# First layer's shift and scale vectors from TensorE column tiles, and no element-wise products on GpSimd, in a four-layer decoder trunk

## The chip, the cores and the metric

One core of a Trainium2 chip runs the whole program in one launch. The metric is device microseconds of one execution, the median of 3 runs.

## The reference, cut to what matters

Four layers work on 256 tokens of 1024 features. Each layer has a token mixer (layers 0 and 3: attention in a window of 128 with rotary positions; layer 1: gated linear attention; layer 2: forgetting attention) and a SwiGLU feed-forward part. Ahead of each part the tokens are normalised and modulated by vectors that come from one conditioning vector `c` and a 1024 x 6144 matrix per layer:

```
mod = silu(c) @ ada_w[i] + ada_b[i]
sh1, sc1, g1, sh2, sc2, g2 = split(mod, 6)
h = rmsnorm(x, gain) * (1 + sc1) + sh1
x = x + g1 * mixer(h)
h = rmsnorm(x, gain') * (1 + sc2) + sh2
x = x + g2 * swiglu(h)
```

So each layer has six modulation vectors of 1024, each the product of `silu(c)` with a 1024 x 1024 block (4 MB). All arithmetic is float32.

## The kernel before, in words

**Stream of weights.** All weights arrive in the order of one list (`items`, L1144), mostly 1 MB at a time, through SyncE's DMA queue into a ring of `RAW` = 5 tiles named `raw` (L94, L180). The load of an item waits until the item five places ahead of it has been used up. There are two kinds. A `w` item is a weight chunk: ScalarE casts it to `wh` (L195) and VectorE takes the remainder `wl = raw - wh` (L197), in two pieces each. An `a` item holds the columns of one modulation vector for 256 features, transposed, so that one feature is one partition row of 1024 numbers.

**Modulation vectors (`ada_pieces`, L201).** An `a` item has two pieces of 128 features. A piece is normally one VectorE instruction (L217): multiply the 128 x 1024 tile by `cact` (`silu(c)` on all partitions), sum along the row, add the bias. For the pieces in `POOL_ADA` (L60, layer 0 only: 18 of its 40 pieces of vectors 0 to 4) GpSimd multiplies (L212), ScalarE sums (L214) and VectorE adds the bias (L215).

**Matrix products** are made of three float32r matmuls each (`mm3`, L258: high x high, high x low, low x high).

**The order at the start (layer 0).** `ORDER0` (L56) lists the first 30 items: `w` chunks of the mixer, `h`, `s`, `g`, `H`, `S` the items of vectors 0 (shift), 1 (scale), 2 (gate), 3 (second shift), 4 (second scale). `first_chunks` (L695) sums the squares of `x` (ScalarE L405, additions on GpSimd L416), takes the norm with small TensorE products (L309, L322, L332), and then works in four rounds `r`. A round forces the items of shift and scale for two of the eight feature tiles, makes the scale column `A` (L361), the two tiles of `h` (VectorE L435 `tk`, ScalarE L437 `hh`, VectorE L430 `hl`), and runs the matmuls of these two tiles for the first two weight chunks (keys, values) as far as their weights are there. In this kernel the first chunk is item 0 and the second item 8.

**The rest of the mixer.** Keys and four groups of queries get the rotary positions (`rope`, L613: VectorE L622, L623, L625, then an addition, L631 for keys and L629 for queries). `ROPE_ADD` (L58) puts these additions on GpSimd in layer 0 and on VectorE in layer 3. Attention (`attn_heads`, L529) runs as a background generator between the matmuls: scores (TensorE L559), masks and minimum (VectorE L572), exponentials (ScalarE L577), division (VectorE L547 and ScalarE L545), transposes (L600), values (TensorE L589, two heads at output partitions 0 to 63 and 64 to 127). GpSimd copies the sink columns (L569, L570). The remaining items of the stream are used up between the matmuls, in shares (`tick`, L226). `out_proj` and the feed-forward part follow.

`Tile`, the layer under this code, draws the waits, and may put an instruction that is ready earlier ahead of others on its engine.

Of the kernel before, what the change touches and what calls it, by code (L numbers as in the profile page):

```python
# [13 lines left out]
AF = mybir.ActivationFunctionType  # L14
ALU = mybir.AluOpType
PSUM = bass.MemoryType.PSUM

P = 128
D = 1024
KT = D // P  # L20
S = 256
# [5 lines left out]
GH = 4  # L27
# [4 lines left out]

CONST_COLS = [
    ("ident", 128), ("ones", 2), ("eps", 1), ("gain", DEPTH * 2 * KT), ("ada_b", DEPTH * 48),
    ("fin", KT), ("hnorm", 2), ("bgate", GH), ("bf", 1),
]
CONST2_COLS = [
    ("cos", NB * HD), ("sin", NB * HD), ("swamask", 3 * P), ("foxmask", 3 * P), ("scan", S),
# [14 lines left out]
WIDE = KT * (256 + 16)  # L53
RAW = 5
MIX_POOL = ((), (), (), ())
ORDER0 = "wshshshhwswwwgwwgggSwHSwHSSHHw"  # L56
BG_SWA = ((1.2, -6.5, 4.5), (0.63, 2.0, 1.6))
ROPE_ADD = (('gpsimd', 'gpsimd'), ('vector', 'vector'))  # L58
EARLY = 2
POOL_ADA = {(0, 0): (0, 1, 2, 4, 5), (0, 1): (7,), (0, 2): (1, 3, 4), (0, 3): (0, 1, 2, 4, 5), (0, 4): (1, 3, 4, 7)}  # L60
CUTS = (2, 2, 2)
OUT_POOL = ()
FFN_POOL = ()
# [80 lines left out]
class Builder:  # L144
# [56 lines left out]
    def ada_pieces(self, it, raw):  # L201

        nc = self.nc
        layer, nt = it[1]
        mod = self.mod[layer]
        bias = self.c("ada_b")[:, layer * 48:(layer + 1) * 48]

        def piece(i):
            w = raw[:, i * D:(i + 1) * D]
            col, b = mod[:, nt + i:nt + i + 1], bias[:, nt + i:nt + i + 1]  # L210
            if (nt + i) % KT in POOL_ADA.get((layer, nt // KT), ()):
                nc.gpsimd.tensor_tensor(out=w, in0=w, in1=self.cact, op=ALU.mult)  # L212
                s = self.t(self.small, [P, 1], "adac", bufs=2)
                nc.scalar.activation(w, w, AF.Copy, accum_out=s)  # L214
                nc.vector.tensor_tensor(out=col, in0=s, in1=b, op=ALU.add)  # L215
            else:
                nc.vector.tensor_tensor_reduce(out=w, in0=w, in1=self.cact, scale=1.0, scalar=b,  # L217
                                               op0=ALU.mult, op1=ALU.add, accum_out=col)
        return [lambda: piece(0), lambda: piece(1)]


    def start_chunk(self, ticks):
# [472 lines left out]
    def first_chunks(self):  # L695

        nc = self.nc
        self.A, self.late = None, []
        self.st.cap = self.st.widx[EARLY]
        self.per_tick = 0.0  # L700
        for k in range(KT):
            self.x_done(k)
        self.stat_start(self.acc)
        self.stat_end()
        self.tc.keep_in_program_order(nc.scalar.dma_start(self.const2, self.a["const2"]))
        rbs = self.t(self.small, [P, S], "rbs", bufs=1)
        nc.scalar.copy(rbs, self.spread(self.y))
        hs = hh, hl = self.h_alloc()
        A = self.t(self.small, [P, KT], "A", bufs=2)
        sh = self.mod[0][:, :KT]  # L710
        outs, ws, todo = [], [], []
        for r in range(4):
            self.st.force_ada(0, (0, 1), r)
            self.mod_cols(0, 0, 2 * r, 2 * r + 2, A)
            self.h_tiles(range(2 * r, 2 * r + 2), rbs, A, sh, hh, hl)
            while len(ws) < EARLY and (r == 3 or self.st.pos[f"i0_{len(ws)}"] < self.st.done):
                c = len(ws)
                ws.append([x.rearrange("p (k n) -> p k n", k=KT) for x in self.st.get(f"i0_{c}")])
                self.st.cap = self.st.widx[EARLY]
                outs.append(self.banks(("mm", "s")[c])[0])  # L720
                todo.append(0)
            for c, (wh, wl) in enumerate(ws):
                for k in range(todo[c], 2 * r + 2):
                    for m in range(2):
                        sl = slice(m * P, (m + 1) * P)
                        self.mm3(outs[c][m][:, :S], hh[:, k, sl], hl[:, k, sl], wh[:, k], wl[:, k],
                                 k == 0, k == KT - 1)
                todo[c] = 2 * r + 2
        return hs, [[o[:, :S] for o in out] for out in outs]
# [482 lines left out]
    def build(self):  # L1212
        nc, tc, ctx = self.nc, self.tc, self.ctx
        pool = lambda n: ctx.enter_context(tc.tile_pool(name=n, bufs=1))
        cp = pool("const")
        self.wpool = pool("w")
        self.hpool = pool("h")
        self.small = pool("small")
        self.psum = ctx.enter_context(tc.tile_pool(name="ps", bufs=1, space=PSUM))

        self.x = self.t(cp, [P, KT, S], "x")
        self.const = self.t(cp, [P, CONST_W], "const")
        self.const2 = self.t(cp, [P, CONST2_W], "const2")
        self.cact = self.t(cp, [P, D], "cact")
        self.mod = [self.t(cp, [P, 48], f"mod{l}") for l in range(DEPTH)]
        self.gla_wg = self.t(cp, [16, GH * P], "gla_wg")
        self.gla_masks = self.t(cp, [P, 7, P], "gla_masks", U8)

        crow = self.t(self.hpool, [P, KT, S], "hh", bufs=1).rearrange("p k n -> p (k n)")[:1, :D]
        nc.sync.dma_start(crow, self.a["c"])  # L1230
        nc.sync.dma_start(self.const, self.a["const"])
        nc.sync.dma_start(self.x, self.a["x"])
        self.st = Stream(self, self.items())
        self.st.issue()
        one = self.t(self.small, [P, S], "fc", bufs=2)[:1, :P]
        nc.vector.memset(one, 1.0)
        for i in range(2):
            ps = self.ps("t")
            sl = slice(i * 512, (i + 1) * 512)
            nc.tensor.matmul(ps, one, crow[:, sl], start=True, stop=True)  # L1240
            nc.scalar.activation(self.cact[:, sl], ps, AF.Silu)

        mixers = [self.swa, self.gla, self.fox]
        for l in range(DEPTH):
            with tc.tile_pool(name=f"mix{l}", bufs=1, reuse_waits="tile") as mp:
                self.layer = l
                self.done_k = 0
                oh = self.t(mp, [P, KT, S], "oh", F32R)
                ol = self.t(mp, [P, KT, S], "ol", F32R)
                self.cuts, self.on_pool = CUTS[0], MIX_POOL[l]  # L1250
                mixers[l % 3](l, oh, ol, mp)
                self.cuts, self.on_pool = CUTS[1], OUT_POOL
                self.out_proj(l, oh, ol, self.mod[l][:, 2 * KT:3 * KT])
            self.cuts, self.on_pool = CUTS[2], FFN_POOL
            self.ffn(l)
        self.final_tile(KT - 1)
        stat = self.ps("o")
        self.stat = [stat[:, b:b + 1] for b in range(NB)]
        self.stat_end(self.acc)
        for i, ps in enumerate(self.final):  # L1260
            o = self.t(self.wpool, [P, WIDE], "raw", bufs=RAW)[:, :512]
            b, half = divmod(i, 2)
            y = self.y[:, b:b + 1]
            if b:
                nc.scalar.activation(o, ps, AF.Copy, scale=y)
            else:
                nc.vector.tensor_scalar(out=o, in0=ps, scalar1=y, scalar2=None, op0=ALU.mult)
            (nc.scalar if b else nc.sync).dma_start(
                self.out[b * P:(b + 1) * P, half * 512:(half + 1) * 512], o)
# [3 lines left out]
def _chunks(w, cols):  # L1273

    k, n = w.shape
    return w.reshape(k // P, P, n // cols, cols).transpose(2, 1, 0, 3).reshape(n // cols, P, -1)
# [8 lines left out]
def _colmajor(v):  # L1285

    return v.reshape(-1, P).T


def _layout(i):  # L1290
    f = np.float32
    a = {}
    a["x"] = i["x"][0].T.reshape(KT, P, S).transpose(1, 0, 2)
    a["c"] = i["c"].reshape(1, D)
    ada = i["ada_w"].reshape(DEPTH, D, 6, D).transpose(0, 2, 3, 1)
    a["ada"] = ada.reshape(DEPTH * 6, 4, 2, P, D).transpose(0, 1, 3, 2, 4).reshape(DEPTH * 6, 4, P, 2 * D)
    gu = i["ffn_w_gu"].reshape(DEPTH, KT, P, 2, FT, P)[:, :, :, :, :2]
    gu = gu.transpose(0, 4, 2, 1, 3, 5).reshape(DEPTH, 2, P, KT * 2 * P)
    gt = i["ffn_w_gu"].reshape(DEPTH, 2, KT // 2, P, 2, FT // 2, 2 * P)[:, :, :, :, :, 1:]
# [8 lines left out]
    w = i["gla_w_in"][0]  # L1308
# [6 lines left out]
    w = i["fox_w_in"][0]  # L1315
# [6 lines left out]
    c, c2 = np.zeros((P, CONST_W), f), np.zeros((P, CONST2_W), f)  # L1322

    def put(name, v):
        lo, hi = COFF[name] if name in COFF else C2OFF[name]
        (c if name in COFF else c2)[:v.shape[0], lo:hi] = v
    put("ident", np.eye(P, dtype=f))
    put("ones", np.tile(np.array([[1.0 / D, 1.0 / 256]], f), (P, 1)))
    put("eps", np.full((P, 1), EPS, f))
    put("gain", _colmajor(i["norm_gain"]))  # L1330
    put("ada_b", _colmajor(i["ada_b"]))
# [19 lines left out]
    s, t = np.arange(P)[:, None], np.arange(P)[None, :]  # L1351
# [22 lines left out]
```

## Time and profile before

| | |
|---|---|
| median of 3 runs (range) | 1269.9 us (1268.44 to 1271.39) |
| the profiled execution | 1267.95 us, span 1266.2 us |
| TensorE matmul busy | 1192.6 us, 94% of the span |
| VectorE busy | 1029.8 us, 81% |
| ScalarE busy | 713.5 us, 56% |
| GpSimd busy | 199.8 us, 16% |
| DMA | 298.5 MB, mean 236 GB/s |

The views that answer for single stretches give busy microseconds of each engine. In a row of a group, the number after the bar is its busy time in us, then the mean of one instruction in ns, then the idle time of the engine in front of it.

### The profile page before, as it was taken

The page shows a single profiled execution, that of the slowest core. Times are in us where ns is not written, and L with a number is a line of the kernel's source. Part 1 is how long each engine was busy: PE and PEld are TensorE (multiplying, and loading weights), DVE is VectorE, ACT ScalarE, POOL GpSimd, SP SyncE. Part 2 cuts the span into 40 slices and gives each one's busy share as a digit, 9 for nine tenths or more (in the row PEclk, how much of TensorE's full clock was granted, in tenths as well). Part 3 has the DMA queues.
Part 4 walks back from the last instruction along what each step waited for, and adds up shares of the span by engine and source line. Part 5 has one row for each costly group of instructions (what it writes and reads, how often), then busy time and mean ns, then how long its engine had stood idle before and what let it go on. Part 6 is the DMA issues. An engine that isn't in the chain of part 4 may idle for free.

```text
span 1266.2 us, 19497 instructions
## 1 busy us (share of the span) xinstructions
PE 1192.6 (94%) x7284; PEld 1046.0 (83%) x7284; DVE 1029.8 (81%) x1815; ACT 713.5 (56%) x1321; POOL 199.8 (16%) x211
## 2 busy tenths in 40 slices
PE   3687889999998999999999999999999999999997
PEld 2575778888898899888889999888888979888886
DVE  5999999988779989988788758998888998766553
ACT  4565764445567747444447867644455677544442
POOL 5456320000104403000012101100002021000011
PEclk9997899999999999999999999999999999999999
DMA  8664579887855335998885653698888544565450
GB/s 333 257 237 167 233 254 358 321 309 263 288 185 200 133 134 172 365 332 313 269 298 201 215 178 124 246 354 328 300 273 282 178 167 158 211 230 199 164 170 34
DMA packets 44673, 298.50 MB, mean 236 GB/s; under 512 B 5169, under 2 KB 5329, under 8 KB 14242
## 3 DMA queue, kind: packets, MB, share of 16 engines
q1 hardware_dynamic: 43778, 295.53, 65.1%
q8 instruction: 57, 0.93, 0.3%
q10 hardware_dynamic: 432, 1.20, 0.2%
q0 software_dynamic: 368, 0.53, 0.1%
q14 instruction: 38, 0.31, 0.1%
HBM read 296.15 MB, written 1.05 MB: 235 GB/s over the span
## 4 chain that ended last, share of the span: by engine, by line
PE 80%; DVE 11%; ACT 3%; issue 3%; POOL 1%; DMA 1%; DVEq 0%; SPq 0%; POOLq 0%; ACTq 0%
PE mm L1113 12%; PE mm L260 11%; PE mm L261 11%; PE mm L262 11%; PE s L261 7%; PE s L260 7%; PE s L262 7%; PE mm L1115 7%; DVE wl L197 3%; DVE raw L217 2%; PE s L559 2%; PE t L1084 1%; PE o L589 1%; DVE pr L547 1%; ACT wh L195 1%
## 5 line engine op out<-in xcount | busy, mean ns | idle before, releaser
L197 DVE TENSOR_TENSOR wl<-raw,wh 128x1024 fp32r<-128x1024 f32 (+2 forms) x408 | 453.8, 1145 | 87.3 <-ACT wh L195 86.2
L195 ACT CAST wh<-raw 128x1024 fp32r<-128x1024 f32 (+2 forms) x408 | 376.1, 964 | 213.9 <-issue 104.9
L1113 PE MATMUL mm<-a,wh 128*128 128x512 f32 x704 | 245.9, 392 | 0.0
L217 DVE CUSTOM_DVE_ANT_0 raw<-raw,cact,const 128x1024 f32<-128x1024 f32 x174 | 232.2, 1351 | 14.1 <-DMA raw<-in_ada 14.1
L260 PE MATMUL mm<-wh,hh 128*128 128x512 f32 (+1 forms) x560 | 199.5, 356 | 20.1 <-ACT hh L437 20.1
L1115 PE MATMUL mm<-a,wl 128*128 128x256 f32 x704 | 198.5, 282 | 0.0
L262 PE MATMUL mm<-wh,hl 128*128 128x512 f32 (+1 forms) x560 | 195.4, 350 | 1.3 <-DVE hl L430 1.3
L261 PE MATMUL mm<-wl,hh 128*128 128x512 f32 (+1 forms) x560 | 194.9, 348 | 0.0
L416 POOL TENSOR_TENSOR sq<-sq,sq 128x256 f32<-128x256 f32 x54 | 58.7, 1086 | 750.4 <-ACT sq L405 718.1
L1113 PEld LDWEIGHTS mm<-a,wh 128*128 128x128 f32 x704 | 132.2, 188 | 27.4
L260 PE MATMUL s<-wh,hh 128*128 128x512 f32 (+2 forms) x384 | 144.9, 379 | 2.9 <-ACT hh L437 2.9
L261 PE MATMUL s<-wl,hh 128*128 128x512 f32 (+2 forms) x384 | 143.1, 374 | 0.2 <-DVE wl L197 0.2
L262 PE MATMUL s<-wh,hl 128*128 128x512 f32 (+2 forms) x384 | 142.4, 374 | 0.0
L260 PEld LDWEIGHTS mm<-wh,hh 128*128 128x128 f32 x560 | 107.8, 193 | 36.0 <-ACT hh L437 21.0
L1115 PEld LDWEIGHTS mm<-a,wl 128*128 128x128 f32 x704 | 133.1, 189 | 0.2
L262 PEld LDWEIGHTS mm<-wh,hl 128*128 128x128 f32 x560 | 107.5, 193 | 15.7 <-DVE hl L430 2.0
L261 PEld LDWEIGHTS mm<-wl,hh 128*128 128x128 f32 x560 | 108.1, 193 | 12.2 <-issue 0.3
L497 DVE SCALAR_TENSOR_TENSOR x<-mm,mod,x 128x256 f32<-128x256 f32 x128 | 61.2, 480 | 41.0 <-PE mm L1115 32.2
L260 PEld LDWEIGHTS s<-wh,hh 128*128 128x128 f32 x384 | 72.6, 189 | 15.2 <-ACT hh L437 3.4
L261 PEld LDWEIGHTS s<-wl,hh 128*128 128x128 f32 x384 | 72.7, 189 | 12.5 <-DVE wl L197 0.5
L262 PEld LDWEIGHTS s<-wh,hl 128*128 128x128 f32 x384 | 72.0, 189 | 13.0
L260 PE MATMUL mm<-oh,wh 128*128 128x256 f32 x256 | 73.2, 291 | 0.4 <-ACT oh L493 0.4
(215 smaller groups left out, 2071.7 us busy)
## 6 DMA issues: line engine op xcount, KB each, us to landing
raw<-in_ada SPq DMA_DIRECT2D x96, 1024.0 KB, 6.3
raw<-in_gu SPq DMA_DIRECT2D x88, 1024.0 KB, 6.5
raw<-in_down SPq DMA_DIRECT2D x64, 704.0 KB, 5.1
raw<-in_swa_in SPq DMA_DIRECT2D x12, 1024.0 KB, 6.8
raw<-in_gla_in SPq DMA_DIRECT2D x11, 1024.0 KB, 5.7
raw<-in_fox_in SPq DMA_DIRECT2D x11, 1024.0 KB, 4.9
raw<-in_swa_o SPq DMA_DIRECT2D x8, 1024.0 KB, 5.0
raw<-in_gla_o SPq DMA_DIRECT2D x4, 1024.0 KB, 4.9
```

The lines of the kernel that those rows point to most:

```text
L195: nc.scalar.copy(wh[:, sl], raw[:, sl])
L197: eng.tensor_tensor(out=wl[:, sl], in0=raw[:, sl], in1=wh[:, sl].bitcast(F32), op=ALU.subtract)
L217: nc.vector.tensor_tensor_reduce(out=w, in0=w, in1=self.cact, scale=1.0, scalar=b, op0=ALU.mult, op1=ALU.add, accum_out=col)
L260: nc.tensor.matmul(out, ah, bh, start=first, stop=False)
L261: nc.tensor.matmul(out, ah, bl, start=False, stop=False)
L262: nc.tensor.matmul(out, al, bh, start=False, stop=last)
L416: (eng or nc.gpsimd).tensor_tensor(out=q, in0=self.acc, in1=q, op=ALU.add)
L497: self.nc.vector.scalar_tensor_tensor(out=self.x[:, m], in0=ps, scalar=gate[:, m:m + 1], in1=self.x[:, m], op0=ALU.mult, op1=ALU.add)
L547: nc.vector.tensor_scalar(out=pr[:, e, 129:385], in0=pr[:, e, 129:385], scalar1=rd[:, 2 * e + 1:2 * e + 2], scalar2=None, op0=ALU.mult)
L559: nc.tensor.matmul(sc[:, so:s1], q[:, so:so + P], k[:, :k1], start=True, stop=True)
L1113: nc.tensor.matmul(o, wh[:, k], a[:, kk].rearrange("p e n -> p (e n)"), start=kk == 0, stop=False)
L1115: nc.tensor.matmul(o[:, S:], wl[:, k], a[:, kk, 0], start=False, stop=kk == FT - 1)
```

## The change

Vectors 0 and 1 of layer 0 are laid out in memory like weight chunks (features of `c` on the partitions, 256 outputs per item). A new function makes one item by eight TensorE products: the stationary operand is a 128 x 32 tile with `silu(c)` in its first column and zeros in the other 31; feature tile `k` goes to output partitions `32 * (k % 4)`. ScalarE copies the 128 x 256 result to SBUF, two one-column products with a column of ones add up the partitions and turn the row into a column, and VectorE adds the bias. The first 10 items come as `shwshshwsh`; the two chunks join in rounds 0 and 2. All other modulation pieces are VectorE's single instruction, the rotary additions of layer 0 and the additions of squares in `first_chunks` are VectorE's as well. A small const column block of `c` and of ones is loaded with the constants.

```diff
-ORDER0 = "wshshshhwswwwgwwgggSwHSwHSSHHw"
+ORDER0 = "shwshshwshwwwgwwgggSwHSwHSSHHw"
-ROPE_ADD = (('gpsimd', 'gpsimd'), ('vector', 'vector'))
+ROPE_ADD = (('vector', 'vector'), ('vector', 'vector'))
-POOL_ADA = {(0, 0): (0, 1, 2, 4, 5), (0, 1): (7,), (0, 2): (1, 3, 4), (0, 3): (0, 1, 2, 4, 5), (0, 4): (1, 3, 4, 7)}
...
+        if layer == 0 and nt < 2 * KT:
+            return self.ada_rows(mod[:, nt:nt + 2], bias[:, nt:nt + 2], raw)
...
-            if (nt + i) % KT in POOL_ADA.get((layer, nt // KT), ()):
-                nc.gpsimd.tensor_tensor(out=w, in0=w, in1=self.cact, op=ALU.mult)
-                s = self.t(self.small, [P, 1], "adac", bufs=2)
-                nc.scalar.activation(w, w, AF.Copy, accum_out=s)
-                nc.vector.tensor_tensor(out=col, in0=s, in1=b, op=ALU.add)
...
+    def ada_rows(self, mod, bias, raw):
+        nc = self.nc
+        w = raw[:, :2048].rearrange("p (k n) -> p k n", k=KT)
+        ps = self.ps("t")
+        row = self.t(self.small, [P, S], "fc", bufs=2)
+
+        def product():
+            for k in range(KT):
+                j = k % 4 * 32
+                nc.tensor.matmul(ps[j:j + 32, :S], self.ccol[:, k], w[:, k], start=k < 4, stop=k >= 4)
+            nc.scalar.copy(row, ps[:, :S])
+
+        def turn():
+            for m in range(2):
+                nc.tensor.matmul(ps[:, S + m:S + m + 1], row[:, m * P:(m + 1) * P], self.c("one"),
+                                 start=True, stop=True)
+            nc.vector.tensor_tensor(out=mod, in0=ps[:, S:S + 2], in1=bias, op=ALU.add)
+        return [product, lambda: self.turns.append(turn)]
...
         for k in range(KT):
-            self.x_done(k)
+            self.x_done(k, nc.vector)
...
             self.st.force_ada(0, (0, 1), r)
+            while self.turns:
+                self.turns.pop(0)()
...
-            while len(ws) < EARLY and (r == 3 or self.st.pos[f"i0_{len(ws)}"] < self.st.done):
+            if r in (0, 2):
...
+        self.ccol = self.t(self.small, [P, KT, 32], "ccol", bufs=1)
+        nc.vector.memset(self.ccol, 0.0)
+        nc.scalar.activation(self.ccol[:, :, 0:1], self.c("c").unsqueeze(2), AF.Silu)
...
+    for v in range(2):
+        a["ada"][v] = _chunks(i["ada_w"][0, :, v * D:(v + 1) * D], 256)
```

## Rows read from the trace of the kernel before

**Rows 1.** Stretches: us, busy us (instructions) PE, PEld, DVE, ACT, POOL, PEclk, DMA share, GB/s.
```profile
0.00:54.00 54.00, 23.19 (x100) 18.64 (x101) 37.02 (x53) 23.43 (x41) 24.23 (x21) 1.00 0.79 300
54.00:131.00 77.00, 60.57 (x417) 48.34 (x416) 73.52 (x151) 47.75 (x125) 49.31 (x50) 0.89 0.55 198
131.00:150.00 19.00, 18.48 (x142) 17.39 (x143) 16.88 (x41) 13.78 (x30) 0.31 (x1) 0.90 0.61 231
170.00:460.00 290.00, 282.01 (x1718) 251.01 (x1717) 250.95 (x448) 164.01 (x273) 45.23 (x43) 1.00 0.70 249
```
**Rows 2.** The chain that ended last, in order of time: start us, us, what.
```profile
38.84 3.30 DVE raw L217
...
54.03 0.40 DVE r L622
...
127.23 4.24 DVE pr L547 x2
...
147.19 0.12 PE mm L260
```
**Rows 3.** Timeline of GpSimd, then VectorE: start us, us, instruction, count.
```profile
7.63 4.73 POOL L416 TENSOR_TENSOR sq<-sq,sq 128x256 f32<-128x256 f32 x6 [5.66 <-ACT sq L405]
95.80 8.01 POOL L212 TENSOR_TENSOR raw<-raw,cact 128x1024 f32<-128x1024 f32 x3
...
50.18 0.16 DVE L361 SCALAR_TENSOR_TENSOR A<-mod,const 128x2 f32<-128x2 f32 x1
99.19 4.77 DVE L547 TENSOR_SCALAR pr<-pr,rd 128x256 f32<-128x256 f32 x2
```
**Rows 4.** Groups of VectorE by line and shape, 54 to 150 us.
```profile
L197 DVE TENSOR_TENSOR wl<-raw,wh 128x1024 fp32r<-128x1024 f32 x16 | 26.4, 1686 | 0.0
L547 DVE TENSOR_SCALAR pr<-pr,rd 128x256 f32<-128x256 f32 x16 | 19.0, 1229 | 0.0
L217 DVE CUSTOM_DVE_ANT_0 raw<-raw,cact,const 128x1024 f32<-128x1024 f32 x12 | 17.3, 1445 | 0.0
```
**Rows 5.** The same view in layer 3's mixer, 960 to 1060 us.
```profile
L197 DVE TENSOR_TENSOR wl<-raw,wh 128x1024 fp32r<-128x1024 f32 x22 | 26.4, 1216 | 1.1 <-ACT wh L195 1.0
L217 DVE CUSTOM_DVE_ANT_0 raw<-raw,cact,const 128x1024 f32<-128x1024 f32 x8 | 10.2, 1272 | 0.0
L547 DVE TENSOR_SCALAR pr<-pr,rd 128x256 f32<-128x256 f32 x16 | 4.9, 347 | 0.0
L629 DVE TENSOR_TENSOR qr<-r,r 128x256 f32<-128x256 f32 x8 | 3.3, 412 | 0.0
```
**Rows 6.** One line's instructions: L215, ns min/median/max, first and last start us.
```profile
L215 DVE TENSOR_TENSOR mod<-adac,const x18: 144/152/2302, 24.2 to 145.0; 128x1 f32<-128x1 f32 x18
```
**Rows 7.** Tile raw on SyncE's queue, 0 to 12 us: first issues, and landing.
```profile
L182 SPq DMA_DIRECT2D raw<-in_ada x4: 432/450/1006, 2.5 to 4.5; - x4
L182 SPq DMA_DIRECT2D raw<-in_swa_in x1: 444/444/444, 2.0 to 2.0; - x1
...
DMA to landing us min/median/max: 7.3/10.3/12.7
```
**Rows 8.** Float32 products on TensorE: timeline (first row), then the chain.
```profile
2.38 3.75 PE L1240 MATMUL t<-hh,fc 1*128 1x512 f32 x4 [2.38 <-DMA hh<-in_c]
...
13.42 0.87 PE t L322 x4
...
111.22 1.48 PE o L589 x8
117.69 0.80 PE o L589 x8
```
**Rows 9.** The chain's matmuls of 256 columns around 49 us.
```profile
49.22 0.21 PE s L261
49.44 0.12 PE s L262
```
**Rows 10.** Groups of ScalarE, 14 to 54 us: a 128x256 copy from PSUM.
```profile
L707 ACT COPY rbs<-t 128x256 f32<-128x256 f32 x1 | 0.4, 372 | 1.5 <-PE t L332 1.5
```

More of the change, by code (lines that the diff above doesn't have):

```diff
@@ L34 @@
     ("ident", 128), ("ones", 2), ("eps", 1), ("gain", DEPTH * 2 * KT), ("ada_b", DEPTH * 48),
-    ("fin", KT), ("hnorm", 2), ("bgate", GH), ("bf", 1),
+    ("fin", KT), ("hnorm", 2), ("bgate", GH), ("bf", 1), ("one", 1), ("c", KT),
 ]
@@ L210, in piece @@
             col, b = mod[:, nt + i:nt + i + 1], bias[:, nt + i:nt + i + 1]
-            if (nt + i) % KT in POOL_ADA.get((layer, nt // KT), ()):
-                nc.gpsimd.tensor_tensor(out=w, in0=w, in1=self.cact, op=ALU.mult)
-                s = self.t(self.small, [P, 1], "adac", bufs=2)
-                nc.scalar.activation(w, w, AF.Copy, accum_out=s)
-                nc.vector.tensor_tensor(out=col, in0=s, in1=b, op=ALU.add)
-            else:
-                nc.vector.tensor_tensor_reduce(out=w, in0=w, in1=self.cact, scale=1.0, scalar=b,
-                                               op0=ALU.mult, op1=ALU.add, accum_out=col)
-        return [lambda: piece(0), lambda: piece(1)]
+            nc.vector.tensor_tensor_reduce(out=w, in0=w, in1=self.cact, scale=1.0, scalar=b,
+                                           op0=ALU.mult, op1=ALU.add, accum_out=col)
+        return [lambda: piece(0), lambda: piece(1)]
+    def ada_rows(self, mod, bias, raw):
[14 more added lines that the diff above has]
+        return [product, lambda: self.turns.append(turn)]
     def start_chunk(self, ticks):
@@ L700, in first_chunks @@
         self.per_tick = 0.0
+        self.turns = []
         for k in range(KT):
-            self.x_done(k)
+            self.x_done(k, nc.vector)
         self.stat_start(self.acc)
@@ L1328, in _layout @@
     put("ones", np.tile(np.array([[1.0 / D, 1.0 / 256]], f), (P, 1)))
+    put("one", np.ones((P, 1), f))
+    put("c", _colmajor(i["c"]))
     put("eps", np.full((P, 1), EPS, f))
```

## The prediction

> **What bounds the kernel now.** I read the busy time by stretches first, then the chain of waits, then the two engines that share a stretch, then the groups by shape.
>
> The stretches [rows 1]: from 170 to 460 us TensorE is busy 282 of 290 us, so whatever the first layer's mixer gives back ahead of that passes to the end, and nothing behind it is changed. Layer 0's mixer is different. From 54 us (first rotary instruction, [rows 2]) to 131 us VectorE is busy 73.5 of 77 us and TensorE 60.6; from 131 to 150 us it is TensorE, 18.5 of 19. Up to 54 us VectorE is busy 37.0 us, nearly all of them after 14 us, and TensorE only 23.2. The chain of waits agrees: VectorE's products (L217, 3.30 us for one) up to 50 us, VectorE's divisions (L547) at 127 us, TensorE's matmuls at 147 us [rows 2].
>
> Why VectorE is long there: three GpSimd products in a row hold 95.8 to 103.8 us, and two divisions beside them take 4.77 us [rows 3]. From 54 to 150 us one division takes 1229 ns, a remainder (L197) 1686 and a product (L217) 1445 [rows 4]. Layer 3's mixer runs the same code with no product and no rotary addition on GpSimd: 347, 1216 and 1272 ns [rows 5]. That is a control inside the same trace.
>
> **The change part by part.** Sums are against the profiled execution, 1267.95 us (span 1266.2 and 1.75 around it); the median is 1.95 us above, and I add that at the end.
>
> *Stretch B, 54 to 150 us.* Removed waits of VectorE: L547 16 x (1229 - 347) = 14.1 us, L197 16 x (1686 - 1216) = 7.5, L217 12 x (1445 - 1272) = 2.1, and one L215 of 2302 against a median of 152 ns, 2.2 [rows 4 to 6]. Together 25.9 us. Part is owed to the rotary additions on GpSimd, which go too. Removed work: 12 additions L215 of 0.15 us, 1.8. Added: 12 products that GpSimd had, 12 x 1.27 = 15.3; eight query additions of 0.412, 3.3; two key additions of double width, at most 2 x 0.82 = 1.6 [rows 5]. Net 25.9 + 1.8 - 20.2 = 7.5 us less. VectorE is idle for 3.5 us up to 131 [rows 1], so I take nearly all, **8 us** with what idle time goes along. Bounds: 4 us if half is lost to waits on ScalarE and TensorE; 13 us if the additions that fall behind 131 us hide beside TensorE (five of the twelve products, 6.4 us). ScalarE loses 12 sums (L214) and nothing waits for them then. GpSimd keeps only the sink copies in the mixer; its queue is never in front of them any more. The products' loads are the same in number and size, so the bytes do not change.
>
> *Stretch A, 0 to 54 us.* Its 16 products (10 on VectorE, six on GpSimd by the list at L60) vanish, so the old chain is gone; what is late next are the loads, TensorE, and a chain of small steps in each round.
>
> Start: the six additions of squares take 4.73 us on GpSimd [rows 3]; on VectorE 6 x 0.412 = 2.5 [rows 5], so the norm's products come 2.2 us earlier than 13.4 + 0.9 [rows 8], and the first product finds its PSUM tile at about 12 us. One memset and one ScalarE instruction for the stationary tile lie ahead, beside the load of `x`, and cost nothing; uncovered they cost under 1 us.
>
> Loads: the first lands at 2.0 + 7.3 = 9.3, the fifth at 4.5 + 12.7 = 17.2, so 2.0 us each [rows 7]; the stretch moved 300 GB/s at a share of 0.79 [rows 1], thus 380 at full share, 2.8 us for 1.05 MB. The tenth load, the last of round 3, lands at 9.3 + 9 x 2.4 = 31, and the second const block (0.67 MB, ScalarE's queue) pushes it to 32.5; bounds 29 and 36. It needs ring places in time: they come free after a TensorE product now, at about 14 us for the first, where before the sixth load waited until 21 us. The SyncE queue holds the next ten chunks behind these; at 2.4 us each they run ahead of VectorE in B.
>
> TensorE: L589 has four matmuls, 768 columns, on two column tiles: 1.48 us at the level of 1.2 GHz, 0.80 at 2.4 [rows 8]. L1240's two, 1024 columns without tiles, took 3.75 at the low level, so 768 would take 2.81: two tiles do run side by side. No row shows four. One product here has 2048 columns: like two tiles 3.95 us low or 2.13 high, like four half of that, 1.97 or 1.07. I take the latter, as overlap by two is nearly complete. Turning one item costs two one-column matmuls, 0.87 / 2 x 2 = 0.87 low [rows 8], half at high. The 96 matmuls of the two chunks go at 0.21 us low, 0.12 high [rows 9]. All: 8 x 1.97 + 8 x 0.87 + 96 x 0.21 = 43 us low; 8 x 1.07 + 8 x 0.44 + 96 x 0.12 = 24 us high. The clock column of that stretch reads 1.00 [rows 1], but 256 columns in 0.21 us are 1.2 GHz; I go by the spacing. TensorE rises to the high level after it was fed steadily from 44 to 49.4 us [rows 9], so here I count some 5 us low, then high.
>
> The switch into column tiles and back is inside L589's 0.80 us: half of L1240's price for 768 columns at the high level is 0.70, so both switches cost 0.1 us or less, under 1 us in all. The Trainium skill (TensorEngine Tiling, Key Properties) says that changing the tiling mode, not just the tile, drains TensorE, which speaks against eight products between untiled ones; it gives no price, and by it the sum gains those eight drains, which the L589 rows bound at under 1 us.
>
> End: after the last load one product 1.1 to 2.0, a copy of 0.37 [rows 10], a turn 0.4 to 0.9, the bias 0.15 [rows 6], and from L361 at 50.2 to the first rotary instruction at 54.0 as before, 3.85 us [rows 2, 3]: 6 to 7.3. That gives 39. TensorE's queue is in order, and at round 2 the second chunk brings 36 + 12 matmuls (5.8 us) ahead of round 3's products: I add half, so A ends at **42 us** instead of 54, 12 us less. Bounds 35 (early loads, no queue) and 47 (late loads, full queue).
>
> Sum: 1267.95 - 12 - 8 = 1248; with 1.95 for the median, **1250 us**.
>
> **The rivals.**
>
> *TensorE stays at 1.2 GHz in A.* The products arrive load by load, with gaps. At 43 us of work from 12 us, A ends at 55, 58 with the tail, 4 us later than before; with B's 8 us: 1266. For it: before, the chunks' matmuls run at 0.21 us until 49.4 [rows 9]. Against it: TensorE was then idle most of the time (23 of 54 us [rows 1]), and a TensorE that is late is a busy one. 13%. The Trainium skill (TensorE: Matmul & The Clock Gate, What's actually happening) has the throttled state as the default and activity as what releases it; rows 9 agree, and by that rule sparse products would keep A at the price of this rival.
>
> *B gives nothing.* The background attention's own chain (scores, exponentials, transposes, values) or TensorE after 131 us ends last. 1270 - 12 = 1258. For it TensorE's 60.6 of 77 us, part at the low level; against it layer 3. 12%.
>
> *Slower: the four column tiles run one after another.* Place: the eight products of A. 2048 columns by L1240's price are 7.5 us low, 3.75 high; A ends between 12 + 30 + 15 = 57 and 12 + 60 + 7 + 20 = 99, so the total lies between 1265 and 1307. Slower from A = 62, a product of 4.3 us or more. L589's rows speak against it. 5%.
>
> *Slower: VectorE's length in B does not come from GpSimd* but from loads or TensorE. Then B grows by 20.2 - 1.8 = 18 us for what stays; with A's 12 this decides when under a quarter of the 25.9 us goes. At none: 1276. Layer 3's rows speak against it. 3%. That the change does not do what it says (TensorE's products put late by the order) would be a form of the first rival.
>
> **How the numbers follow.** The forecast has 67%; its own range runs from 1238 (A ends at 35 and B gives 13, 32 us together) to 1259 (A ends at 47 and B gives 4, 11 us). To hold 8 in 10 it must take in the rivals at 1258 and 1266: **1238 to 1266**. A measurement of this kernel can tell about 0.2%, 2.5 us: faster is under 1267.4. Faster 0.89, same 0.05 (the first rival a little worse), slower 0.06.
>
> **What would show it.** First rotary instruction (L622) at 42 us; one tiled product about 1.1 us from start to next once matmuls go at 0.12 us; the tenth load at 32 us; L547 near 350 ns and L197 near 1220 in the first mixer; VectorE's busy time between L622 and 150 us of old some 8 us less; the matmuls of `out_proj` (147 us before) some 20 us earlier, and the rest of the trace unchanged but shifted. Wrong: L622 after 50, products above 2 us, or long divisions beside an idle GpSimd.

## The result: 1262.3 us, and the profile after

| | before | after |
|---|---|---|
| median (range) of 5 runs each | 1269.9 us (1268.44 to 1271.39) | 1262.28 us (1260.51 to 1265.44) |
| the profiled execution | 1267.95 us, span 1266.2 | 1260.51 us, span 1258.7 |
| VectorE busy | 1029.8 us | 1000.2 us |
| GpSimd busy | 199.8 us | 136.3 us |

The ratio is 0.995, interval 0.9934 to 0.9966 (the two medians give 0.994): faster by 7.6 us, inside the range of 1238 to 1266, but not the 20 us forecast. Where the two profiled executions part, in us from the span's start (timeline):

| | first rotary instruction | first tile `a` of layer 0's feed-forward part | layer 1's mixer starts | layer 2's mixer starts | span |
|---|---|---|---|---|---|
| before | 54.03 | 178.00 | 349.65 | 694.09 | 1266.2 |
| after | 52.71 | 167.18 | 339.70 | 685.89 | 1258.7 |
| earlier by | 1.3 | 10.8 | 10.0 | 8.2 | 7.5 |

So in this execution A, the stretch up to the first rotary instruction, was to give 12 us and gave 1.3; B, taken here from there to the first tile `a`, was to give 8 and gave 10.8 - 1.3 = 9.5; and 3.3 us were lost again behind that tile, where nothing was to change. The profiled execution is the fastest of the five, and its A is not that of every execution (see the clock, below).

The stretches of the changed kernel, for [rows 1] with A cut finer (the columns are those of [rows 1]):

```profile
14.00:22.00 8.00, 5.17 (x43) 2.70 (x42) 1.30 (x7) 2.37 (x5) 0.93 (x4) 0.95 1.01 425
22.00:26.00 4.00, 3.56 (x16) 2.92 (x20) 3.11 (x5) 1.53 (x3) 0.09 (x1) 0.50 0.73 307
26.00:35.00 9.00, 7.04 (x59) 4.70 (x55) 2.25 (x7) 1.65 (x4) 0.00 (x0) 0.69 0.92 342
35.00:43.00 8.00, 5.40 (x57) 3.87 (x50) 3.94 (x9) 3.54 (x6) 0.00 (x0) 1.00 0.73 264
43.00:53.00 10.00, 8.96 (x86) 7.73 (x86) 3.12 (x9) 3.33 (x6) 0.00 (x0) 0.95 0.71 248
54.00:131.00 77.00, 68.86 (x496) 56.95 (x495) 71.26 (x192) 45.42 (x126) 11.57 (x28) 0.92 0.60 215
123.00:137.00 14.00, 7.96 (x52) 7.22 (x50) 14.00 (x25) 5.58 (x7) 0.00 (x0) 0.88 0.90 339
170.00:460.00 290.00, 281.46 (x1724) 250.27 (x1723) 247.44 (x453) 160.93 (x267) 39.55 (x41) 0.99 0.68 247
```

VectorE is nearly free in A now: 13.7 us of the 39 from 14 to 53. But neither TensorE (30.1 of 39) nor the loads, past 22 us, are full. That is how a chain looks in which each engine waits for another. The chain of waits names the links (start us, us, what; compare [rows 2]):

```profile
12.83 7.97 DMA const<-in_const
...
25.74 1.91 PE t L228 x16
27.73 0.38 ACT fc L229
28.15 0.61 PE t L233 x4
28.76 1.04 PE t L228 x16
29.88 0.38 ACT fc L229
30.31 0.62 PE t L233 x4
31.21 0.52 ACT hh L454
31.77 0.58 PE mm L277
...
34.70 1.17 PE t L228 x16
...
46.93 1.86 PE t L228 x32
```

Read one round, from 25.7 to 34.7 us: product of the scale item (L228), ScalarE's copy (L229), turn (L233), product of the shift item, copy, turn, `hh` (L454), 12 matmuls (L277 to L279), and only then the next round's first product. None of these links overlaps another. The four rounds begin at 14.5, 25.7, 34.6 and 46.9 us. The last row is round 3's products. Their data had been there for 10 us (compare [rows 7]; one line's instructions on SyncE's queue, ns min/median/max, first and last start, then the time to landing):

```profile
L181 SPq DMA_DIRECT2D raw<-in_ada x8: 327/380/475, 2.0 to 29.8; - x8
...
DMA to landing us min/median/max: 4.9/6.9/12.6
```

The last of these loads was issued at 29.8 us and landed 6.9 later, at 36.7 by the timeline. The waits from 14 to 53 us (who waited <- for whom: us in total, times, longest) say the same:

```profile
DVE mod L235 <- PE t L233: 21.1, 6, 5.8
ACT fc L229 <- PE t L228: 20.7, 8, 5.8
...
PEld mm L277 <- ACT hh L454: 6.2, 4, 3.2
```

ScalarE and VectorE wait for TensorE's products and turns, TensorE waits for `hh`, and the loads wait too: SyncE's queue stood 23.3 us in seven waits, up to 60 us, for L228 to free a ring place.

```profile
SPq L181 <- PE t L228: 23.3, 7, 7.0
```

B went as forecast. Its VectorE groups, 53 to 150 us, for [rows 4]:

```profile
L213 DVE CUSTOM_DVE_ANT_0 raw<-raw,cact,const 128x1024 f32<-128x1024 f32 x24 | 30.0, 1282 | 0.0
L196 DVE TENSOR_TENSOR wl<-raw,wh 128x1024 fp32r<-128x1024 f32 x20 | 24.6, 1262 | 0.0
...
L564 DVE TENSOR_SCALAR pr<-pr,rd 128x256 f32<-128x256 f32 x16 | 4.9, 354 | 0.0
...
L646 DVE TENSOR_TENSOR qr<-r,r 128x256 f32<-128x256 f32 x8 | 3.4, 422 | 0.0
```

A division takes 354 ns where it took 1229, a remainder 1262 for 1686, a product 1282 for 1445: the durations of the layer-3 control [rows 5]. From the first rotary instruction to the first tile `a`, VectorE was busy 116.97 us before and 107.41 after, 9.6 less, and the stretch is 9.5 shorter.

### The profile page after: what moved, and what is told of

It reads as the page before. It is cut to its first block, busy times and chain, and to the rows that moved or that the text cites. A ratio compares the mean times of both kernels' runs of the same rounds, so it can differ in the third digit from the quotient of the medians.

```text
span 1258.7 us, 19761 instructions
## 1 busy us (share of the span) xinstructions
PE 1207.7 (96%) x7444; PEld 1053.3 (84%) x7444; DVE 1000.2 (79%) x1826; ACT 698.3 (55%) x1294; POOL 136.3 (11%) x177
## 4 chain that ended last, share of the span: by engine, by line
PE 84%; DVE 7%; ACT 4%; issue 2%; DMA 2%; POOL 1%; DVEq 0%; SPq 0%; ACTq 0%; POOLq 0%
PE mm L1133 13%; PE mm L277 12%; PE mm L278 11%; PE mm L279 11%; PE s L278 7%; PE s L277 7%; PE s L279 7%; PE mm L1135 7%; PE s L576 2%; DVE wl L196 2%; PE o L606 2%; DVE raw L213 1%; PE t L1104 1%; PE t L617 1%; ACT wh L194 1%
## 5 line engine op out<-in xcount | busy, mean ns | idle before, releaser
L196 DVE TENSOR_TENSOR wl<-raw,wh 128x1024 fp32r<-128x1024 f32 (+2 forms) x408 | 447.2, 1129 | 88.0 <-ACT wh L194 86.9
L213 DVE CUSTOM_DVE_ANT_0 raw<-raw,cact,const 128x1024 f32<-128x1024 f32 x176 | 224.1, 1292 | 11.2 <-DMA raw<-in_ada 11.1
L277 PE MATMUL mm<-wh,hh 128*128 128x512 f32 (+1 forms) x560 | 198.8, 356 | 6.1 <-ACT hh L454 5.8
L279 PE MATMUL mm<-wh,hl 128*128 128x512 f32 (+1 forms) x560 | 193.5, 347 | 0.0
L277 PE MATMUL s<-wh,hh 128*128 128x512 f32 (+2 forms) x384 | 145.1, 379 | 2.9 <-ACT hh L454 2.9
L279 PE MATMUL s<-wh,hl 128*128 128x512 f32 (+2 forms) x384 | 142.1, 374 | 0.0
L433 POOL TENSOR_TENSOR sq<-sq,sq 128x256 f32<-128x256 f32 x48 | 53.9, 1123 | 758.4 <-ACT sq L422 732.2
L277 PEld LDWEIGHTS mm<-wh,hh 128*128 128x128 f32 x560 | 107.0, 191 | 21.3 <-ACT hh L454 6.2
L279 PEld LDWEIGHTS mm<-wh,hl 128*128 128x128 f32 x560 | 106.9, 192 | 13.0 <-issue 0.2
L514 DVE SCALAR_TENSOR_TENSOR x<-mm,mod,x 128x256 f32<-128x256 f32 x128 | 61.5, 481 | 44.7 <-PE mm L1135 37.5
L277 PEld LDWEIGHTS s<-wh,hh 128*128 128x128 f32 x384 | 72.5, 189 | 15.5 <-ACT hh L454 3.4
L279 PEld LDWEIGHTS s<-wh,hl 128*128 128x128 f32 x384 | 72.2, 190 | 13.1
L277 PE MATMUL mm<-oh,wh 128*128 128x256 f32 x256 | 74.8, 297 | 8.3 <-DVE x L514 8.2
```

What stands on the lines that cost most here:

```text
L196: eng.tensor_tensor(out=wl[:, sl], in0=raw[:, sl], in1=wh[:, sl].bitcast(F32), op=ALU.subtract)
L277: nc.tensor.matmul(out, ah, bh, start=first, stop=False)
L279: nc.tensor.matmul(out, al, bh, start=False, stop=last)
L433: (eng or nc.gpsimd).tensor_tensor(out=q, in0=self.acc, in1=q, op=ALU.add)
L514: self.nc.vector.scalar_tensor_tensor(out=self.x[:, m], in0=ps, scalar=gate[:, m:m + 1], in1=self.x[:, m], op0=ALU.mult, op1=ALU.add)
```

## The experiments

Twelve kernels ran. Ratios are against runs of the kernel before on the same chip (medians 1269.56 to 1270.16 us). "Rotary" is the start of the first rotary instruction in the profiled execution, the end of A.

### Are the rounds the missing time?

Theory 1: the rounds stand one behind another in TensorE's queue, which works in order. The first kernel issues each round's two products ahead of the previous round's matmuls and fixes TensorE's order there; the second, a control, fixes the order and leaves the products where they were.

```diff
         for r in range(4):
-            self.st.force_ada(0, (0, 1), r)
+            if r == 0:
+                self.st.force_ada(0, (0, 1), 0)
             while self.turns:
                 self.turns.pop(0)()
...
+            if r < 3:
+                self.st.force_ada(0, (0, 1), r + 1)
             for c, (wh, wl) in enumerate(ws):
...
-                                 k == 0, k == KT - 1)
+                                 k == 0, k == KT - 1, pin=True)
```

`pin` passes the three matmuls of `mm3` through `keep_in_program_order`, as the products and turns are; that last edit with those is the whole of the control.

> The changed kernel, but each round's TensorE products are issued ahead of the matmuls of the round before (and TensorE's instructions of the four rounds are kept in the order of the program). Theory 1: stretch A is long because the four rounds follow one another on TensorE's in-order queue: products, copy, turn, bias, tiles of h, matmuls, and only then the next round's products, though their loads have long landed (the tenth at 36.7 us, its product at 47). Then the first rotary instruction comes at 43 to 46 us instead of 52.7, and the kernel takes 1253 to 1256 us instead of 1262.3. Theory 2: the loads bound A, since a ring place comes free late. Then the first rotary instruction stays within 2 us of 52.7 and the time within 2 us of 1262. Theory 3: TensorE at 1.2 GHz bounds it; then some 3 us are gained, 1259.

> The control for the first experiment: TensorE's instructions of the four rounds are kept in the order of the program, but each round's products stay behind the matmuls of the round before, as in the changed kernel. The two products of a round then stand next to each other in all rounds. If it is the place of the products ahead of the matmuls that helped: first rotary instruction at 51 to 52, 1260 to 1262 us. If it was only that both products stand together: near 46.4 and 1255 as in the first experiment.

Measured: products early 1255.34 us, ratio 0.9899 (0.9865 to 0.9933), rotary at 46.42 us, just past the edge expected. The control 1263.77, 0.9952 (0.9935 to 0.9968), rotary at 53.23. So it is the place of the products. TensorE's timeline of the first kernel (start us, us, line, shape, count, wait in front):

```profile
19.54 1.07 PE L229 MATMUL t<-raw,ccol 128*32 128x256 f32 x16
21.80 1.07 PE L229 MATMUL t<-raw,ccol 128*32 128x256 f32 x16 [1.19 <-DVE mod L237]
...
25.89 1.93 PE L229 MATMUL t<-raw,ccol 128*32 128x256 f32 x32
...
35.16 1.48 PE L229 MATMUL t<-raw,ccol 128*32 128x256 f32 x16 [0.52 <-DMA raw<-in_ada]
...
42.42 0.95 PE L235 MATMUL t<-const,fc 128*128 128x1 f32 x8
```

Rounds 1 and 2 have their products at 19.5 and 25.9 us instead of 25.7 and 34.6, and now it is TensorE that waits for a load. Ring places come free earlier, so the DMA share from 14 to 46 us is 0.97 where the change has 0.83. Part of the gain may be the clock that a busier TensorE gets: from 22 to 26 us it is 1.00 here and 0.50 in the change.

### What holds the start of round 0?

In the chain above A begins with `const`, not with a product. VectorE's queue has, behind the bias of the first scale item, an instruction that waits for the second const block:

```profile
20.83 0.18 DVE L690 TENSOR_SCALAR nsink<-const 128x16 f32<-128x16 f32 x1 [1.98 <-DMA const<-in_const]
```

The experiment puts the sinks, all that it needs, into the first block.

```diff
-    ("fin", KT), ("hnorm", 2), ("bgate", GH), ("bf", 1), ("one", 1), ("c", KT),
+    ("fin", KT), ("hnorm", 2), ("bgate", GH), ("bf", 1), ("one", 1), ("c", KT), ("sinks", 2 * 16),
...
-    ("sinks", 2 * 16),
```

> The changed kernel, with the sinks' column in the first block of constants, so that the instruction that negates them no longer waits for the second block. In the changed kernel VectorE stood still from 18.9 to 20.8 us behind that instruction. Theory 1 (a chain of rounds): round 0 starts 2 us earlier and all of it passes on: the first rotary instruction at 50.7, 1260 us. Theory 2 (loads): nothing passes on, 52.7 and 1262 us.

Measured: 1261.12 us, 0.993 (0.9906 to 0.9955), not told apart from the change. Round 0's matmuls did begin at 19.98 instead of 22.25 us, but the rotary instruction came at 53.80, not earlier. Its stretches show TensorE at a granted clock of 0.50, 1.2 GHz, from 35 to 43 us, where the change had 1.00:

```profile
26.00:35.00 9.00, 7.04 (x52) 4.73 (x51) 2.25 (x7) 1.65 (x4) 0.00 (x0) 0.61 0.70 287
35.00:43.00 8.00, 6.59 (x38) 5.15 (x39) 3.93 (x9) 3.16 (x5) 0.00 (x0) 0.50 0.75 262
```

The stall is real. What it costs, this run cannot say, because the clock moved the other way.

### Is it the clock?

The control's order, with TensorE filled: 128-column matmuls of the constant `ident` with itself into a PSUM tile that nobody reads (added work, the kernel's own is unchanged).

```diff
+    def fill(self, n):
+        for _ in range(n):
+            self.tc.keep_in_program_order(self.nc.tensor.matmul(
+                self.dummy[:, :P], self.c("ident"), self.c("ident"), start=True, stop=True))
...
+        self.fill(11)
         self.A, self.late = None, []
...
+            self.fill(2)
             while self.turns:
                 self.turns.pop(0)()
+            self.fill(5)
```

> The kernel of the fifth experiment, with TensorE's idle times filled: 11 products of the identity with itself (128 columns, float32) ahead of the sums of squares, 2 between a round's products and its turns, 5 between the turns and the matmuls. They compute nothing that is used. If the level of 1.2 GHz in A is a large part (theory 3), the products and matmuls of rounds 0 and 1 go at 2.4 GHz: first rotary instruction 3 to 5 us earlier than without, at 47 to 49, 1256 to 1258 us, and the runs lie closer together than the 7 to 9 us of the changed kernels so far. If not, nothing is gained, or up to 2 us are lost to the filling itself.

Measured: 1258.57 us, 0.9915 (0.99 to 0.993), rotary at 51.80 us. The clock from 26 to 43 us is 1.00 (first two rows), where the control has 0.69, then 0.78 (last two):

```profile
26.00:35.00 9.00, 8.75 (x105) 6.41 (x97) 2.15 (x7) 2.40 (x6) 0.00 (x0) 1.00 0.90 343
35.00:43.00 8.00, 7.25 (x56) 6.65 (x57) 4.51 (x9) 2.79 (x4) 0.00 (x0) 1.00 0.75 280
...
26.00:35.00 9.00, 7.93 (x64) 5.14 (x66) 2.15 (x7) 1.65 (x4) 0.00 (x0) 0.69 0.91 331
35.00:43.00 8.00, 6.96 (x59) 5.96 (x52) 4.52 (x9) 3.54 (x6) 0.00 (x0) 0.78 0.72 276
```

A is 1.4 us shorter than the control's, not the 3 to 5 expected: round 3's products still begin at 44.20, behind everything of round 2. The total gains more, 5.2 us against the control. In the two traces the rest lies behind A: from the rotary instruction to the first tile `a` it is 111.5 us against 115.4; why is open. So the clock is a cost of A, but a high clock doesn't mend the order: with products early, and no filling, A ended 5.4 us sooner still.

How large it can be showed in another run, that of the second shift and scale below. Its first 54 us have the order of the change, and its TensorE never rose between 22 and 43 us:

```profile
22.00:26.00 4.00, 3.74 (x20) 2.99 (x24) 2.93 (x4) 1.35 (x3) 0.00 (x0) 0.50 0.84 309
26.00:35.00 9.00, 7.05 (x48) 4.50 (x41) 2.25 (x7) 1.65 (x4) 0.00 (x0) 0.50 0.89 340
35.00:43.00 8.00, 6.91 (x46) 3.94 (x45) 1.20 (x4) 0.74 (x2) 0.00 (x0) 0.50 0.44 147
```

There A ended at 57.74 us, 5.0 later than in the change: the very price of the first rival, 58. The spacing of the matmuls agrees with the column: 256 columns take 0.21 us there, and 0.12 at a granted clock of 1.00. Two more kernels, those of A alone below, have this order too: A ends at 52.62 us in the one, with 1.00 from 35 to 43 us as in the change, and at 56.17 in the other, with 0.50. One order of instructions thus has an A between 52.6 and 57.7 us, long where TensorE stayed at 1.2 GHz. The Trainium skill (TensorE: Matmul & The Clock Gate, What's actually happening) has the throttled state as the default and activity as what releases it; these runs agree, the sparse rounds at 0.50 and, from 26 us on, the filled ones at 1.00.

### A and B apart

B alone is the kernel before with GpSimd's list cut to the vectors of A and the rotary additions on VectorE. A alone is the change with GpSimd's products of vectors 2 to 4 and its rotary additions put back, once with four tiles for its sums, then with two, as before.

```diff
-ROPE_ADD = (('gpsimd', 'gpsimd'), ('vector', 'vector'))
+ROPE_ADD = (('vector', 'vector'), ('vector', 'vector'))
...
-POOL_ADA = {(0, 0): (0, 1, 2, 4, 5), (0, 1): (7,), (0, 2): (1, 3, 4), (0, 3): (0, 1, 2, 4, 5), (0, 4): (1, 3, 4, 7)}
+POOL_ADA = {(0, 0): (0, 1, 2, 4, 5), (0, 1): (7,)}
```

```diff
-ROPE_ADD = (('vector', 'vector'), ('vector', 'vector'))
+ROPE_ADD = (('gpsimd', 'gpsimd'), ('vector', 'vector'))
+POOL_ADA = {(0, 2): (1, 3, 4), (0, 3): (0, 1, 2, 4, 5), (0, 4): (1, 3, 4, 7)}
...
+                s = self.t(self.small, [P, 1], "fcol", bufs=4)
```

In the last kernel both this ring and its other use at L496 have `bufs=2`.

> The kernel before, with only the changes behind stretch A: no GpSimd products for vectors 2, 3 and 4, rotary additions on VectorE; shift and scale as before on VectorE and GpSimd. Theory 1: stretch B alone gives what was forecast for it, 8 us: 1262 us, as much as the whole change. Theory 2 (the parts need one another, for instance because B's loads come earlier by A's order): 3 us or less, 1267 or more.

> The changed kernel, with the GpSimd products of vectors 2, 3 and 4 and the GpSimd rotary additions put back. Theory 1: A alone gives the 1.3 us by which the first rotary instruction came earlier: 1268 to 1269 us. Theory 2: 1262 to 1265, A's order is what helps B.

> The fourth experiment again, with two tiles for GpSimd's sums as in the kernel before, where the fourth experiment had four (its 1263.9 us came with a stretch A that was no shorter in the trace, so the gain lay behind it). If the four tiles gave that gain: 1267 to 1270 us now, and stretch A alone gives nothing. If it is A's order of loads: 1262 to 1266 again.

Measured: B alone 1259.76 us, 0.9931 (0.9907 to 0.9955), as fast as the whole change. Its rotary instruction comes at 54.46, no earlier than before, and its VectorE groups from 53 to 150 us have the durations of layer 3:

```profile
L217 DVE CUSTOM_DVE_ANT_0 raw<-raw,cact,const 128x1024 f32<-128x1024 f32 x24 | 30.0, 1283 | 0.0
L197 DVE TENSOR_TENSOR wl<-raw,wh 128x1024 fp32r<-128x1024 f32 x19 | 23.0, 1245 | 0.0
...
L547 DVE TENSOR_SCALAR pr<-pr,rd 128x256 f32<-128x256 f32 x16 | 4.9, 355 | 0.0
```

A alone with four tiles 1263.9, 0.9948 (0.9932 to 0.9964), a surprise, since the A of its trace was no shorter (rotary at 56.17; the profiled execution is the slowest of ten, 1267.82). With two tiles 1268.76, 0.9998 (0.9981 to 1.0015): nothing, though the A of its trace ends at 52.62. The 5 us of the first form came with the two more tiles for GpSimd's sums, not from A: in the traces the way from the rotary instruction to the first tile `a` is 117.8 us with four tiles and 124.6 with two (124.0 before). How two tiles do that was not tested. (The ring is shared with layer 2's mixer, which shows no cost of it: 389.71 us from its start to the last feed-forward part, 389.63 before.) So the change's whole gain is B's. Which part of GpSimd's work B owes it to, products or rotary additions, these runs do not separate.

### Early products, filled, without the sinks' wait

The first, second and filling edits together.

> All three together: products a round early, TensorE filled, sinks in the first constants. With the rounds overlapped, TensorE at the high level and no stall of VectorE, only the loads and their ring places are left in A: first rotary instruction at 41 to 44, 1249 to 1253 us, that is the end of A that was forecast at 42. If A stays at 46 or later, something else bounds it (the loads' ring places).

Measured: 1250.65 us, 0.9859 (0.983 to 0.9889), rotary at 45.54. TensorE's timeline:

```profile
20.78 1.39 PE L228 MATMUL t<-raw,ccol 128*32 128x256 f32 x16 [2.00 <-DMA raw<-in_ada]
...
33.31 1.93 PE L228 MATMUL t<-raw,ccol 128*32 128x256 f32 x32
...
41.47 0.95 PE L234 MATMUL t<-const,fc 128*128 128x1 f32 x8
```

The 45.54 lies between the two outcomes expected. The loads now run without a pause (share 1.00 from 14 to 46 us, 412 GB/s), and round 3's products start at 33.3, where the prediction had its tenth load at 32. Their turn comes only at 41.5: between the two stand round 2's 48 matmuls, from 35.18 to 41.02 us. That is the prediction's 5.8 us, in full and not by half.

### The second shift and scale

After the change VectorE makes the products of vectors 3 and 4 in one burst: it is busy 14.00 of 14 us from 123 to 137, ten products L213, with `x` (L514), for which TensorE waits 8.2 us in four waits from 100 to 140 us, between them. Here these two vectors also go over TensorE's tiles.

```diff
-        if layer == 0 and nt < 2 * KT:
-            return self.ada_rows(mod[:, nt:nt + 2], bias[:, nt:nt + 2], raw)
+        if layer == 0 and nt // KT in ROWS:
+            return self.ada_rows(mod[:, nt:nt + 2], bias[:, nt:nt + 2], raw, nt < 2 * KT)
...
+ROWS = (0, 1, 3, 4)
```

> The changed kernel, with vectors 3 and 4 (second shift and scale of layer 0) made on TensorE in the same way, so the row of ten VectorE products from 123 to 137 us, beside which TensorE was busy 7 of 15 us, is gone. Stretch A is untouched (first rotary instruction 52 to 54). If that row holds the end of the mixer: 4 to 8 us less, 1255 to 1258 us. If attention or the matmuls end last there anyway: within 2 us of 1262.

Measured: 1256.27 us, 0.9889 (0.9865 to 0.9914), 6 us under the change by the medians, though the profiled execution had the slow A. From 125 to 135 us VectorE is busy 2.0 of 10 us and TensorE all 10:

```profile
125.00:130.00 5.00, 5.00 (x57) 3.69 (x57) 1.20 (x5) 0.75 (x2) 0.00 (x0) 1.00 0.94 365
130.00:135.00 5.00, 5.00 (x56) 3.48 (x54) 0.83 (x5) 1.20 (x3) 0.00 (x0) 1.00 1.00 359
```

From the rotary instruction to the first tile `a` the trace has 109.2 us where the change had 114.5.

### Put together, and the values last

First the kernel of the early products, filling and sinks with the edit of the second shift and scale; then the same with the values chunk moved behind the shift and scale items and into round 3 (the diff); then that without filling (`fill(0)` in all three places).

```diff
-ORDER0 = "shwshshwshwwwgwwgggSwHSwHSSHHw"
+ORDER0 = "shwshshshwwwwgwwgggSwHSwHSSHHw"
...
-            if r in (0, 2):
+            if r in (0, 3):
```

> The seventh and the eighth experiment together: products a round early, TensorE filled, sinks in the first constants, and second shift and scale on TensorE too. The two work in different stretches, so their gains add: the seventh's 1250.7 less the eighth's 6, 1243 to 1246 us, first rotary instruction at 44 to 46. If the end of the mixer is held by something common (loads at full rate): 1249 to 1251.

> The tenth, with the second chunk (values) loaded as the last of the ten items and all its 48 matmuls behind the first chunk's in round 3, so the keys' rotary instructions need not wait for the 36 matmuls that round 2 brings. First rotary instruction at 41 to 43, that is 3 us earlier; the total 1 to 3 us below the tenth, since the values are needed only by the attention. If the loads hold A: first rotary instruction within 1 us of the tenth and the same time.

> The eleventh without the filling matmuls. If TensorE needs them to stay at 2.4 GHz even with rounds overlapped: 3 to 5 us slower than the eleventh and with a wider spread. If the overlapped rounds keep it fed: within 2 us.

Measured: together 1244.37 us, 0.9791 (0.9769 to 0.9814), rotary at 45.79; values last 1243.24, 0.9792 (0.9764 to 0.982), rotary at 41.13; unfilled 1244.72, 0.98 (0.9769 to 0.9832), rotary at 39.61. The gains add up (1250.65 less the 6 of the second shift and scale is 1244.6). With the values last A ends where the prediction had put the change, 41.1 for 42, yet the total hardly moves. The stretches of the kernel put together show a reason: behind A, TensorE is full to the end of layer 0's mixer.

```profile
45.79:100.00 54.21, 53.87 (x428) 43.76 (x426) 50.30 (x153) 39.65 (x106) 6.93 (x26) 1.00 0.63 230
100.00:142.64 42.64, 42.00 (x390) 36.19 (x390) 28.28 (x63) 26.34 (x62) 6.84 (x9) 1.00 0.69 254
```

An earlier end of A that only puts the values' matmuls off moves work from one full stretch into the next. All three beat both kernels, by 25 to 26 us and 18 to 19 us. With the values last, the kernels with and without filling are not told apart (ranges 1242.86 to 1247.89 and 1242.5 to 1249.69).

## Why the prediction was wrong in size

**Luck in the range.** The time lies inside the stated range only because that was widened to 1266 for the rivals. The forecast's own range ended at 1259, and of its two gains one came and the other did not.

**Stretch B: right.** Forecast 8 us with bounds 4 and 13; measured 9.5 in the profiled execution, and B alone gives 0.9931. Every duration taken from layer 3 came out within 4% ([rows 5] against 354, 1262, 1282 and 422 ns). GpSimd's work beside VectorE was the cost, as read; both rivals that denied it fell.

**Stretch A, single prices: right, but for the turn.** One tiled product took 1.94 us low and 1.07 high, forecast 1.97 and 1.07; a turn 0.60 high for 0.44, and 1.01 low for 0.87. A product that follows a turn starts with it (28.15 + 0.61, then 28.76 in the chain), so the switch into tiles costs under 0.1 us by the modelled ends, as the L589 rows had bounded it. The rival in which the four tiles run one after another fell. The Trainium skill (TensorEngine Tiling, Key Properties) has a drain of TensorE at each change of the tiling mode; if there is one, it is inside these gaps.

**Stretch A, the end: wrong, and this is the step that failed.** The prediction wrote: "TensorE's queue is in order, and at round 2 the second chunk brings 36 + 12 matmuls (5.8 us) ahead of round 3's products: I add half, so A ends at 42 us". The order was seen, but priced as one half-delay at one place, behind a pipeline that otherwise runs at the pace of the loads. There is no pipeline. In the code the products of round `r` stand behind all matmuls of round `r - 1`, and in the trace the second product of rounds 1 and 2 stands behind the first's copy and turn. So a round is the sum of its links, 9 to 12 us each, and round 3's products began at 46.9 us, where the sum had the load at 32.5 and half the queue, 2.9 us, behind it. Even the upper bound of 47 had only late loads and one full queue in it (its terms, 36, 6 to 7.3 and 5.8 us, add up to 48 or 49). The same order holds the ring: the last load landed at 36.7, past its bound of 36. The start was mis-sized too, if by less: the first product began at 14.50 us, not at 12, behind the norm's last product (L349, 13.34 to 14.57).

The runs size it. Overlapping the rounds takes A from 53.2 to 46.4 (early products against their control), and 5.4 us of that remain against the filled control, whose clock was 1.00 from 26 us. Taking the sinks' wait away and filling as well brings 45.5, moving round 2's second chunk away 41.1. The 42 us were within reach of this scheme, but not of this order.

**The rival of 1.2 GHz** was given 13% and is partly true. The profiled A of the change has 0.50 from 22 to 26 us and 0.69 to 35; another kernel's execution of the same order shows the rival's whole price. "A TensorE that is late is a busy one" was wrong here: it is late because it waits for copies, biases and `hh`.

**Not foreseen:** the wait of L690 for the second const block, about 2 us at the head of round 0 that before hid behind VectorE's long products; and the burst of ten products, which the prediction booked as 12 x 1.27 us of VectorE work without asking where they would stand. Making vectors 3 and 4 on TensorE instead, which removes the burst, gave 6 us.

**"The rest of the trace unchanged but shifted": not quite.** 3.3 of the 10.8 us gained are lost again behind the first tile `a` of layer 0's feed-forward part: 0.9 us up to layer 1's mixer, 1.7 from there to layer 2's mixer, 0.7 later. B alone shows the same 1.8 us in layer 1 (346.23 us against 344.44 before). The kernel with the values last shows none there (344.58) but loses as much in the next stretch, from layer 2's mixer to the last feed-forward part (391.46 us against 389.63). No run was aimed at it, and its cause stays open.

## What to carry to other kernels

Before work moves onto an engine that works its queue in order, write out that queue, and ask of each new instruction what stands ahead of it and what that waits for: here a stage fed load by load came near the pace of the loads only when its products were issued ahead of the previous stage's dependent work. Where a forecast adds up two gains, test each alone: here one gave everything and the other nothing. And where the same code runs elsewhere in the trace without the suspected neighbour, as layer 3 did here, its durations are a good price: they held within 4%.

## What the runs showed of the hardware

- Four column tiles of 32 run side by side almost completely: 2048 float32 columns in 1.94 us at the low level, where the price of the untiled L1240 [rows 8] gives 7.5.
- The start of this kernel has no one length: in four traces the same order of instructions had an A of 52.6, 52.7, 56.2 and 57.7 us, with TensorE at 2.4 GHz from 35 to 43 us in the first two and at 1.2 GHz in the others. How far the totals follow is open. The ten runs of A alone with four tiles go from 1259.12 us (mean granted clock 0.987) to 1267.82 (0.980), but of the change's five runs 1260.51 us came with 0.986 and 1265.18 with 0.987.
- VectorE is slower beside GpSimd's element-wise work: a division of 128 x 256 takes 1229 ns [rows 4] and 354 with that work gone, a remainder of 128 x 1024 1686 and 1262.
- Two more tiles in a small ring, for GpSimd's sums, gave 5 us of 1269, half of what B gave.
